# Low parts of the attention's weight slabs written as two pieces of 128x512 on VectorE and four of 128x256 on GpSimd

## The chip, the cores and the metric

The kernel runs on one core of one Trainium2 chip. The metric is the device time of one execution in microseconds (us). The core has TensorE (PE in the profile, with its weight loads shown apart as PEld), VectorE (DVE), ScalarE (ACT), GpSimd (POOL) and the queue that issues transfers (SP). [...] A change of 0.2% (about 4.7 us here) is about what a measurement of this kernel can tell from no change.

## The reference

A trunk of two layers works on 512 latent and 256 context tokens of width 1024. The part that matters here is the differential attention of each layer:

```python
px = hx @ w_in[i]
q_x = px[..., Q_OFF:K_OFF].reshape(B, S, N_HEADS, 2, QK_DIM)
k_x = px[..., K_OFF:V_OFF].reshape(B, S, N_HEADS, 2, QK_DIM)
v_x = px[..., V_OFF:GATE_OFF].reshape(B, S, N_HEADS, V_DIM)
q_x = apply_rope(rmsnorm(q_x, q_norm_g[i]), cos, sin)
k_x = apply_rope(rmsnorm(k_x, k_norm_g[i]), cos, sin)
...
s = jnp.einsum('bqhcd,bkhcd->bhcqk', qi, keys) * scale
p = jax.nn.softmax(s, axis=-1)
w = p[:, :, 0] - lam * p[:, :, 1]
return jnp.einsum('bhqk,bkhv->bqhv', w, vals)
```

Eight heads, two softmax maps a head, everything in float32. Around it lie a conditioning network (adaLN), a convolution branch, a gated merge of both branches with an output projection, and a squared-ReLU MLP of width 4096. Context tokens take part in layer 0 in full; in layer 1 only their keys and values are needed.

## The kernel before

**Numbers in two parts.** A float32 matrix product is made of three faster ones. Each operand X is split into a high part, which ScalarE writes as a rounded copy, and a low part X minus high, a subtraction of two tensors in SBUF. `mm3` (lines 108 to 111) then adds high x high, high x low and low x high in PSUM; these are the matmuls of L109, L110 and L111.

**Weight slabs.** `load_slab` (line 86) brings 1024 rows x 256 columns of a weight matrix into SBUF as a tile of 128 partitions x 8 x 256 (`r_...`), and makes `h_...` and `l_...` from it. It does so in two halves of 128x1024: for each, one ScalarE copy (L76) and one subtraction (L77). The engine of the subtraction is an argument. The attention asks for `both`, a pair: the first half's low part is written by VectorE, the second half's by GpSimd. This holds for the query and key slab of heads 1 to 7 (`qk_slab(i, h, both)`, tiles `l_wqk`) and the value slab of pairs 1 to 3 (`v_slab(i, pr, both)`, tiles `l_wv`): ten slabs in a layer, twenty in all. All other slabs name one engine or none (VectorE).

**One head.** While TensorE runs the attention of head h (`attend`), it also projects head h+1 (`qk_head`) and, for one pair of heads in two, the values (`v_pair`); a list of costs in microseconds (`merge`, the numbers behind `yield`) mixes the two streams. A projected block of 128 tokens goes through ScalarE (`rw`, L542, and its square, L545), VectorE (sum, L547), GpSimd (power -0.5, `rqk`, L548), GpSimd or VectorE (`rw` scaled, L549), GpSimd (`ra` and `rb` for the rotation, L557 and L561), then two sums `dup` (L566: one on GpSimd, one on VectorE), and back to TensorE, which transposes them (`qkT`, L580); L584, L585 and L587 move the result out of PSUM. Scores `S` (L708, L710) live in two PSUM tiles in turn; a third waits until VectorE's maximum (`st`, L712) and ScalarE's exponential (`e`, L715) have read the first. After the combination of both maps (L725), TensorE transposes the weights (`wT`, L738), and ScalarE and VectorE split them (`wth`, `wtl`).

**What sets the order.** The Tile framework draws up the order of each engine's instructions before the kernel runs, by simulating the whole program against modelled durations. Nothing is reordered at run time. Splitting an instruction changes the modelled times, and so the order of others far from it.

Of the kernel before, what the change touches and what calls it, by code (L numbers as in the profile page):

```python
# [10 lines left out]
AF = mybir.ActivationFunctionType  # L11
ALU = mybir.AluOpType
# [34 lines left out]
def f32(ap):  # L47
    return ap.bitcast(F32)
# [3 lines left out]
def trunk_kernel(  # L52
# [6 lines left out]
    nc = tc.nc  # L59
# [15 lines left out]
    def split(hi, lo, src, lo_eng=None):  # L75
        nc.scalar.activation(out=hi, in_=src, func=AF.Copy)  # L76
        return (lo_eng or nc.vector).tensor_tensor(out=lo, in0=src, in1=f32(hi), op=ALU.subtract)  # L77
# [6 lines left out]
    def load_slab(src, name, shape=(KT, 256), lo_eng=None):  # L84
        r = state["tp"].tile([P, *shape], F32, tag="raw", name=f"r_{name}", bufs=state["nraw"])
        if isinstance(src, (list, tuple)):
            for dst, s in src:
                nc.sync.dma_start(r[:, :, dst], s)
        else:
            state["load"] = nc.sync.dma_start(r, src)  # L90
        hi = wpool.tile([P, *shape], F32R, tag="whi", name=f"h_{name}")
        lo = wpool.tile([P, *shape], F32R, tag="wlo", name=f"l_{name}")
        half = shape[0] // 2
        engs = lo_eng if isinstance(lo_eng, tuple) else (lo_eng, lo_eng)
        with ExitStack() as behind:
            for ins in state["behind"]:
                behind.enter_context(tc.issue_after(ins))
            for n, (k, eng) in enumerate(zip((slice(0, half), slice(half, shape[0])), engs)):
                if n and state["turn"]:
                    behind.enter_context(tc.issue_after(state["turn"]))  # L100
                split(hi[:, k], lo[:, k], r[:, k], eng)
        return hi, lo

    def rows(src, col0, ncols):
# [37 lines left out]
    both = nc.vector, nc.gpsimd  # L142
    first = {}

    def qk_slab(i, h, lo_eng=None):
        return load_slab([(slice(0, P), rows(w_in[i], Q_OFF + h * P, P)),
                          (slice(P, 256), rows(w_in[i], K_OFF + h * P, P))], f"wqk{i}_{h}",
                         lo_eng=lo_eng)

    def v_slab(i, pr, lo_eng=None):  # L150
        return load_slab(rows(w_in[i], V_OFF + 256 * pr, 256), f"wv{i}_{pr}", lo_eng=lo_eng)
# [228 lines left out]
    for t in range(NTT):  # L380
        xn = xns[t]
        nc.scalar.activation(out=xn, in_=xrs[t], func=AF.Square, accum_out=rs[:, t : t + 1])
        r = rs[:, t : t + 1]
# [9 lines left out]
    for s in range(2):  # L393
        nc.vector.tensor_tensor(
            out=cvec[:, :, s], in0=L["cols"][:, R_C + 8 * s : R_C + 8 * s + 8],
            in1=sg[:, 8 * s : 8 * s + 8], op=ALU.mult)
# [38 lines left out]
    for i in range(DEPTH):  # L435
# [27 lines left out]
        def conv_load(part, s):  # L463
            return load_slab(rows(wi, (CW if part == "g" else 0) + 256 * s, 256), f"wc{part}{i}_{s}")
# [598 lines left out]
        for s in range(4):  # L1063
# [3 lines left out]
            for g in groups:  # L1067
                W = g.stop - g.start
                for m in range(2):
# [4 lines left out]
                                            op=ALU.mult)  # L1074
# [12 lines left out]
        for cc in range(CT):  # L1087
            for a0, W, t0 in cgr:
                low = nc.vector.tensor_tensor(out=CL[:, cc, t0 : t0 + W],
                                              in0=ca[cc][:, a0 : a0 + W],  # L1090
                                              in1=f32(CH[:, cc, t0 : t0 + W]), op=ALU.subtract)
        normed.append(low.ins)
        mh, ml = [None] * KT, [None] * KT
        for s in range(2):
# [7 lines left out]
            for m in range(4):  # L1102
                mb = 4 * s + m
                for g in groups:
# [5 lines left out]
                                            op=ALU.mult)  # L1110
                rr = {}
                for g in groups:
# [3 lines left out]
                                            op=ALU.add)  # L1116
# [255 lines left out]
```

## Time and profile before

| | us |
|---|---|
| median of 3 runs | 2361.62 (2360.18 to 2363.51) |
| the profiled execution | 2362.06 |
| its span, from first to last instruction | 2360.0 |
| TensorE busy in the span | 2288.2 (97%) |
| VectorE busy | 1468.9 (62%) |
| GpSimd busy | 684.2 (29%) |

The profiled execution lies 0.44 us over the median, and 2.06 us of it lie outside the span. The attention of layer 0 runs from about 50 to 440 us of the span, that of layer 1 from about 1415 to 1760 us; the twenty slabs in question are all made there. Between them lie the merge, the MLP and the conditioning of the next layer.

A row of a timeline gives the start, the duration, the engine, the line, the operation and the tiles, and in square brackets how long the engine stood idle ahead of it and what ended that. Consecutive matmuls overlap, so the bracket, and not the distance between rows, tells TensorE's idle time.

### The profile page before, as it was taken

The numbers are of one execution on the slowest core, as the hardware profiler recorded it, in microseconds if no ns is written. First come the engines' busy times: TensorE is split into PE (matmuls) and PEld (weight loads), VectorE is DVE, ScalarE is ACT, GpSimd is POOL, SyncE is SP. The second block draws the span as 40 slices with busy tenths as digits, with TensorE's granted clock in tenths as the row PEclk, the third lists the DMA queues.
The fourth block names the chain that finished last, engine by engine and source line by source line (L and its number), as shares of the span: only waits on it lengthen the run. The fifth ranks groups of instructions, "written<-read, shape, count | busy, mean of one in ns | idle before, by whom it ended". The sixth has DMA issues, their size and how long they took to land.

```text
span 2360.0 us, 36545 instructions
## 1 busy us (share of the span) xinstructions
PE 2288.2 (97%) x14698; PEld 2051.8 (87%) x14698; DVE 1468.9 (62%) x2583; ACT 993.2 (42%) x1965; POOL 684.2 (29%) x790
## 2 busy tenths in 40 slices
PE   8999999999999999999999998999999999999999
PEld 6999998888888988888888998999877879888887
DVE  6777776699666675655463366776759975433332
ACT  5555654522332353342514345555542333432432
POOL 1866754100000133232322255766610000000000
PEclk9999999999999999999999999999999999999999
DMA  9211111144535223334332211111124324223322
GB/s 313 57 43 31 44 46 44 46 159 131 178 114 188 88 84 125 116 109 132 116 118 71 99 46 56 44 43 44 42 78 130 122 89 126 88 92 95 102 89 72
DMA packets 222570, 224.76 MB, mean 95 GB/s; under 512 B 6256, under 2 KB 212544, under 8 KB 222272
## 3 DMA queue, kind: packets, MB, share of 16 engines
q1 hardware_dynamic: 222400, 222.43, 29.5%
q8 instruction: 115, 1.88, 0.3%
q14 instruction: 55, 0.45, 0.1%
HBM read 208.73 MB, written 13.67 MB: 94 GB/s over the span
## 4 chain that ended last, share of the span: by engine, by line
PE 84%; DVE 7%; ACT 3%; POOL 2%; DMA 1%; issue 1%; SPq 0%; ACTq 0%; DVEq 0%; POOLq 0%
PE r L109 6%; PE r L110 6%; PE r L111 6%; PE f L110 6%; PE f L109 6%; PE f L111 6%; PE gt L109 3%; PE gt L111 3%; PE gt L110 3%; PE qk L109 2%; PE qk L110 2%; PE qk L111 2%; PE v L109 2%; PE v L110 2%; PE v L111 2%; PE o L111 2%
## 5 line engine op out<-in xcount | busy, mean ns | idle before, releaser
L110 PE MATMUL f<-h2l,h_w 128*128 128x512 f32 (+1 forms) x832 | 284.5, 343 | 3.6 <-DVE h2l L328 2.0
L109 PE MATMUL f<-h2h,h_w 128*128 128x512 f32 (+1 forms) x832 | 282.5, 344 | 2.0 <-ACT h2h L76 1.3
L109 PE MATMUL r<-fh,h_w 128*128 128x512 f32 (+1 forms) x832 | 283.9, 342 | 0.0
L110 PE MATMUL r<-fl,h_w 128*128 128x512 f32 (+1 forms) x832 | 283.0, 340 | 0.0
L111 PE MATMUL r<-fh,l_w 128*128 128x512 f32 (+1 forms) x832 | 282.9, 340 | 0.0
L111 PE MATMUL f<-h2h,l_w 128*128 128x512 f32 (+1 forms) x832 | 282.8, 342 | 0.0
L77 POOL TENSOR_TENSOR l_w<-r_w,h_w 128x1024 fp32r<-128x1024 f32 x64 | 156.7, 2471 | 346.9 <-ACT h_w L76 346.9
L76 ACT ACTIVATE h_w<-r_w 128x1024 fp32r<-128x1024 f32 x128 | 128.5, 1051 | 261.3 <-PE r L110 117.2
L263 DVE SCALAR_TENSOR_TENSOR adaac<-ar,cvec,adaac 128x256 f32<-128x256 f32 x336 | 176.7, 579 | 83.9 <-DMA ar<-in_w_ada_dram 62.0
L945 DVE SCALAR_TENSOR_TENSOR cacc<-z,cols,cacc 128x783 f32<-128x783 f32 (+1 forms) x240 | 201.4, 891 | 0.3
L109 PE MATMUL qk<-h_wqk,h1h 128*128 128x256 f32 x640 | 183.6, 289 | 2.1 <-ACT rw L542 1.4
L110 PE MATMUL qk<-l_wqk,h1h 128*128 128x256 f32 x640 | 180.7, 285 | 0.0
L110 PEld LDWEIGHTS f<-h2l,h_w 128*128 128x128 f32 x832 | 158.8, 191 | 22.7 <-POOL h2l L77 2.9
L111 PE MATMUL qk<-h_wqk,h1l 128*128 128x256 f32 x640 | 176.9, 285 | 0.2 <-POOL h1l L77 0.2
L712 DVE TENSOR_REDUCE st<-S 128x1 f32<-128x768 f32 (+1 forms) x160 | 134.7, 846 | 65.4 <-PE S L710 64.4
L1140 DVE SCALAR_TENSOR_TENSOR X<-r,ad,X 128x512 f32<-128x512 f32 (+1 forms) x104 | 64.8, 625 | 176.8 <-PE r L111 176.7
L109 PEld LDWEIGHTS f<-h2h,h_w 128*128 128x128 f32 x832 | 157.0, 191 | 20.4 <-ACT h2h L76 1.7
L111 PEld LDWEIGHTS f<-h2h,l_w 128*128 128x128 f32 x832 | 158.6, 191 | 17.7
L111 PEld LDWEIGHTS r<-fh,l_w 128*128 128x128 f32 x832 | 157.6, 190 | 17.8
L109 PEld LDWEIGHTS r<-fh,h_w 128*128 128x128 f32 x832 | 157.6, 190 | 17.2
L110 PEld LDWEIGHTS r<-fl,h_w 128*128 128x128 f32 x832 | 157.8, 190 | 16.9
L715 ACT ACTIVATE e<-S,st 128x768 f32<-128x768 f32 (+1 forms) x160 | 130.8, 820 | 36.6 <-DVE st L712 36.5
(253 smaller groups left out, 6240.4 us busy)
## 6 DMA issues: line engine op xcount, KB each, us to landing
r_w<-in_w_mlp_dram SPq DMA_DIRECT2D x64, 1024.0 KB, 5.5
ada<-in_w_ada_dram SPq DMA_DIRECT2D x24, 1024.0 KB, 5.4
ar<-in_w_ada_dram SPq DMA_DIRECT2D x48, 512.0 KB, 3.7
r_wqk<-in_w_in_dram SPq DMA_DIRECT2D x32, 512.0 KB, 5.4
r_wg<-in_w_in_dram SPq DMA_DIRECT2D x16, 1024.0 KB, 5.4
r_wv<-in_w_in_dram SPq DMA_DIRECT2D x8, 1024.0 KB, 5.3
r_wao<-in_w_attn_out_dram SPq DMA_DIRECT2D x8, 1024.0 KB, 5.4
r_wo<-in_w_out_dram SPq DMA_DIRECT2D x8, 1024.0 KB, 8.2
```

The source lines that it names most:

```text
L76: nc.scalar.activation(out=hi, in_=src, func=AF.Copy)
L77: return (lo_eng or nc.vector).tensor_tensor(out=lo, in0=src, in1=f32(hi), op=ALU.subtract)
L109: nc.tensor.matmul(ps, sh, mh, start=first, stop=False)
L110: nc.tensor.matmul(ps, sh, ml, start=False, stop=False)
L111: nc.tensor.matmul(ps, sl, mh, start=False, stop=last)
L263: nc.vector.scalar_tensor_tensor(out=a[:, q], in0=r[:, j], scalar=cvec[:, k, q : q + 1], in1=a[:, q], op0=ALU.mult, op1=ALU.add)
L712: nc.vector.tensor_reduce(out=st[:, m : m + 1], in_=S[:, :nkey], axis=AX.X, op=ALU.max, negate=True)
L715: nc.scalar.activation(out=e[:, :nkey], in_=S[:, :nkey], func=AF.Exp, bias=st[:, m : m + 1], accum_out=st[:, 2 + m : 3 + m])
L945: nc.vector.scalar_tensor_tensor(out=ca[cc][:, :CV], in0=zt[cc][:, t : t + CV], scalar=wcol, in1=ca[cc][:, :CV], op0=ALU.mult, op1=ALU.add)
L1140: nc.vector.scalar_tensor_tensor(out=X[:, mb, g], in0=ps[:, :W], scalar=gate[:, s, mb : mb + 1], in1=X[:, mb, g], op0=ALU.mult, op1=ALU.add)
```

## The change

In `load_slab`, slabs whose engines are the pair `both` no longer call `split`. The ScalarE copies stay as they are. VectorE's subtraction of 128x1024 becomes two of 128x512 (two of the slab's eight blocks at a time), GpSimd's becomes four of 128x256 (one block each). The values written are the same.

```diff
             for n, (k, eng) in enumerate(zip((slice(0, half), slice(half, shape[0])), engs)):
                 if n and state["turn"]:
                     behind.enter_context(tc.issue_after(state["turn"]))
-                split(hi[:, k], lo[:, k], r[:, k], eng)
+                if lo_eng is not both:
+                    split(hi[:, k], lo[:, k], r[:, k], eng)
+                    continue
+
+                nc.scalar.activation(out=hi[:, k], in_=r[:, k], func=AF.Copy)
+                step = 2 if n == 0 else 1
+                for k0 in range(k.start, k.stop, step):
+                    p = slice(k0, k0 + step)
+                    eng.tensor_tensor(out=lo[:, p], in0=r[:, p], in1=f32(hi[:, p]),
+                                      op=ALU.subtract)
```

In the program, 20 instructions of VectorE become 40 and 20 of GpSimd become 80; every other instruction is still there. Lines behind the edit move down by nine (L566 becomes L575), and the new subtractions are L109. With few exceptions the pieces of one half stand directly behind each other (`x2`, `x4`). The order around them is drawn up anew, most of all in the attention of layer 0, and at its start in layer 1. Names in the rows below end in a number that the program gives each tile.

**Scores of the first head, TensorE.** `S_0_0_1` and `S_0_1_0` are the second score tile of the first 128 tokens and the first one of the next 128. In layer 0 before:

```order
L708 MATMUL S_0_0_1_1106<-qk_0_708 128x256
L710 MATMUL S_0_0_1_1106<-qk_0_708 128x256
L708 MATMUL S_0_1_0_1159<-qk_0_708 128x512
L710 MATMUL S_0_1_0_1159<-qk_0_708 128x512
L708 MATMUL S_0_1_0_1159<-qk_0_708 128x256
L710 MATMUL S_0_1_0_1159<-qk_0_708 128x256
```

and now:

```order
L717 MATMUL S_0_0_1_1110<-qk_0_708 128x256
L719 MATMUL S_0_0_1_1110<-qk_0_708 128x256
L589 MATMUL qkT_1_0_1184<-cst,dup_1_0_1033 128x128 x4
L118 MATMUL qk_1_3_1192<-h_wqk_1_990,h1h_334 128x256
L119 MATMUL qk_1_3_1192<-l_wqk_1_991,h1h_334 128x256
L120 MATMUL qk_1_3_1192<-h_wqk_1_990,h1l_335 128x256
```

`S_0_1_0` no longer follows at once; the transposes and 18 matmuls of a projection stand between. In layer 1 before:

```order
L708 MATMUL S_0_0_0_15015<-qk_0_14613 128x256
L710 MATMUL S_0_0_0_15015<-qk_0_14613 128x256
L708 MATMUL S_0_0_1_15023<-qk_0_14613 128x256
L710 MATMUL S_0_0_1_15023<-qk_0_14613 128x256
L580 MATMUL qkT_1_0_15075<-cst,dup_1_0_14947 128x128 x4
L109 MATMUL qk_1_3_15105<-h_wqk_1_14908,h1h_9377 128x256
L110 MATMUL qk_1_3_15105<-l_wqk_1_14909,h1h_9377 128x256
L111 MATMUL qk_1_3_15105<-h_wqk_1_14908,h1l_9378 128x256
```

and now:

```order
L717 MATMUL S_0_0_1_15067<-qk_0_14653 128x256
L719 MATMUL S_0_0_1_15067<-qk_0_14653 128x256
L717 MATMUL S_0_1_0_15128<-qk_0_14653 128x512
L719 MATMUL S_0_1_0_15128<-qk_0_14653 128x512
L717 MATMUL S_0_1_0_15128<-qk_0_14653 128x256
L719 MATMUL S_0_1_0_15128<-qk_0_14653 128x256
L589 MATMUL qkT_1_0_15119<-cst,dup_1_0_14991 128x128 x4
```

Here it is the other way round: `S_0_1_0` now follows at once where a whole projection of 24 matmuls stood between.

**The slab of head 2 in layer 1, VectorE and GpSimd.** VectorE before:

```order
L725 SCALAR_TENSOR_TENSOR e_0_1_15090<-e_0_1_15098,st_0_1_15083,e_0_1_15090 128x768
L712 TENSOR_REDUCE st_0_2_15208<-S_0_2_0_15209 128x1
L77 TENSOR_TENSOR l_wqk_2_15461<-r_wqk_2_15457,h_wqk_2_15460 128x1024
L712 TENSOR_REDUCE st_0_2_15208<-S_0_2_1_15217 128x1
L566 TENSOR_TENSOR dup_1_3_15136<-ra_1_3_15137,rb_1_3_15138 128x4x64
L585 TENSOR_TENSOR qk_1_14914<-qkT_1_2_15230,qk_1_14914 128x2x128
L587 TENSOR_TENSOR qk_1_14914<-qkT_1_2_15230,qk_1_14914 64x2x128
```

and now:

```order
L596 TENSOR_TENSOR qk_1_14958<-qkT_1_1_15200,qk_1_14958 64x2x128
L721 TENSOR_REDUCE st_0_2_15252<-S_0_2_1_15261 128x1
L109 TENSOR_TENSOR l_wqk_2_15509<-r_wqk_2_15505,h_wqk_2_15508 128x512 x2
L575 TENSOR_TENSOR dup_1_3_15180<-ra_1_3_15181,rb_1_3_15182 128x4x64
L77 TENSOR_TENSOR wtl_0_0_1_15056<-wT_0_0_1_15194,wth_0_0_1_15055 128x3x128
L594 TENSOR_TENSOR qk_1_14958<-qkT_1_2_15274,qk_1_14958 128x2x128
L596 TENSOR_TENSOR qk_1_14958<-qkT_1_2_15274,qk_1_14958 64x2x128
```

The two halves stand back to back, behind both maxima of `S_0_2` where the whole subtraction stood between them, and `dup_1_3` follows directly. GpSimd at the same place before:

```order
L724 TENSOR_SCALAR es_0_0_15013<-st_0_1_15083 128x1
L557 TENSOR_TENSOR ra_1_3_15137<-rw_1_3_15130,tC_9351 128x256
L561 TENSOR_TENSOR rb_1_3_15138<-rw_1_3_15130,tS_9352 128x4x32 x2
L77 TENSOR_TENSOR l_wqk_2_15461<-r_wqk_2_15457,h_wqk_2_15460 128x1024
L566 TENSOR_TENSOR dup_1_3_15136<-ra_1_3_15137,rb_1_3_15138 128x4x64
L722 TENSOR_TENSOR st_0_2_15208<-st_0_2_15208 128x1
```

and now:

```order
L566 TENSOR_TENSOR ra_1_3_15181<-rw_1_3_15174,tC_9391 128x256
L570 TENSOR_TENSOR rb_1_3_15182<-rw_1_3_15174,tS_9392 128x4x32 x2
L109 TENSOR_TENSOR l_wqk_2_15509<-r_wqk_2_15505,h_wqk_2_15508 128x256 x4
L575 TENSOR_TENSOR dup_1_3_15180<-ra_1_3_15181,rb_1_3_15182 128x4x64
L731 TENSOR_TENSOR st_0_2_15252<-st_0_2_15252 128x1
L733 TENSOR_SCALAR es_0_1_15251<-st_0_2_15252 128x1
```

The four quarters take the place of the one, between `rb_1_3` and `dup_1_3`.

**The slab of head 5 in layer 1, VectorE.** Before:

```order
L725 SCALAR_TENSOR_TENSOR e_3_2_16787<-e_3_2_16795,st_3_2_16780,e_3_2_16787 128x768
L77 TENSOR_TENSOR l_wqk_5_17058<-r_wqk_5_17054,h_wqk_5_17057 128x1024
L712 TENSOR_REDUCE st_3_3_16912<-S_3_3_1_16921 128x1
L566 TENSOR_TENSOR dup_4_3_16755<-ra_4_3_16756,rb_4_3_16757 128x4x64
L585 TENSOR_TENSOR qk_4_16534<-qkT_4_2_16861,qk_4_16534 128x2x128
L587 TENSOR_TENSOR qk_4_16534<-qkT_4_2_16861,qk_4_16534 64x2x128
```

and now:

```order
L734 SCALAR_TENSOR_TENSOR e_3_2_16851<-e_3_2_16859,st_3_2_16844,e_3_2_16851 128x768
L109 TENSOR_TENSOR l_wqk_5_17122<-r_wqk_5_17118,h_wqk_5_17121 128x512 x2
L721 TENSOR_REDUCE st_3_3_16976<-S_3_3_1_16985 128x1
L575 TENSOR_TENSOR dup_4_3_16819<-ra_4_3_16820,rb_4_3_16821 128x4x64
L594 TENSOR_TENSOR qk_4_16598<-qkT_4_2_16925,qk_4_16598 128x2x128
L596 TENSOR_TENSOR qk_4_16598<-qkT_4_2_16925,qk_4_16598 64x2x128
```

Only the subtraction itself has changed; what stands ahead of it and behind it is the same. The slabs of heads 3 and 7 lie in the same surroundings.

## Rows read from the trace of the kernel before

**Rows 1.** The page's first part: busy us of each engine, share, instructions.
```profile
PE 2288.2 (97%) x14698; PEld 2051.8 (87%) x14698; DVE 1468.9 (62%) x2583; ACT 993.2 (42%) x1965; POOL 684.2 (29%) x790
```

**Rows 2.** Windows: stretch, length, busy of PE, PEld, DVE, ACT, POOL; clock; DMA.
```profile
50.00:440.00 390.00, 378.86 (x2919) 363.34 (x2918) 283.78 (x563) 220.91 (x546) 239.25 (x348) 0.99 0.16 47
...
1415.00:1760.00 345.00, 325.09 (x2390) 306.23 (x2389) 232.92 (x404) 187.11 (x416) 203.72 (x280) 0.98 0.16 49
```

**Rows 3.** Waits of PE, 55 to 430 us: total us, times, longest.
```profile
PE S L708 <- ACT e L715: 3.7, 3, 1.8
...
PE qkT L580 <- POOL dup L569: 2.0, 4, 1.3
PE wT L738 <- DVE wtl L77: 1.7, 3, 0.9
```

**Rows 4.** Waits of PE, 1420 to 1760 us.
```profile
PE v L109 <- DVE qk L587: 5.9, 3, 2.5
PE v L109 <- DVE vl L77: 3.0, 2, 2.5
```

**Rows 5.** Tile l_wqk: who waited for it (us, times).
```profile
who waited for it (us, times):
  PEld adaps L221: 0.3, 1
```

**Rows 6.** Line L77 by form: ns min/median/max, first and last start.
```profile
L77 POOL TENSOR_TENSOR l_w<-r_w,h_w x64: 2379/2402/2697, 816.9 to 1349.3; 128x1024 fp32r<-128x1024 f32 x64
...
L77 DVE TENSOR_TENSOR h1l<-ar,h1h x20: 681/684/694, 625.4 to 1886.1; 128x512 fp32r<-128x512 f32 x20
...
L77 DVE TENSOR_TENSOR l_wqk<-r_wqk,h_wqk x14: 1207/1222/1773, 61.7 to 1662.9; 128x1024 fp32r<-128x1024 f32 x14
L77 POOL TENSOR_TENSOR h1l<-nu_n,h1h x12: 733/740/912, 1369.8 to 1416.3; 128x256 fp32r<-128x256 f32 x12
```

**Rows 7.** Tile dup, its VectorE form: ns min/median/max, first and last start.
```profile
L566 DVE TENSOR_TENSOR dup<-ra,rb x64: 404/426/2586, 64.6 to 1707.5; 128x256 f32<-128x256 f32 x64
```

**Rows 8.** Timelines of POOL, DVE and PE around 1452 us, and DVE at 66.
```profile
1452.13 2.40 POOL L77 TENSOR_TENSOR l_wqk<-r_wqk,h_wqk 128x1024 fp32r<-128x1024 f32 x1
...
1452.22 2.59 DVE L566 TENSOR_TENSOR dup<-ra,rb 128x256 f32<-128x256 f32 x1
...
1459.40 0.44 PE L109 MATMUL v<-h_wv,h1h 128*128 128x256 f32 x1 [2.51 <-DVE vl L77]
...
66.37 2.54 DVE L566 TENSOR_TENSOR dup<-ra,rb 128x256 f32<-128x256 f32 x1
```

**Rows 9.** The chain that ended last, 1579 to 1583 us: start, us, what.
```profile
1579.22 1.48 DVE l_wqk L77
1580.70 0.87 DVE st L712
1581.57 0.53 DVE dup L566
...
1582.44 0.44 DVE qk L587
...
1583.02 0.55 PE v L109
```

**Rows 10.** Timeline of POOL at 153 to 159 us, and at 1578 us.
```profile
153.56 1.50 POOL L549 TENSOR_TENSOR rw<-rw,rqk 128x256 f32<-128x256 f32 x1
...
156.52 2.41 POOL L77 TENSOR_TENSOR l_wqk<-r_wqk,h_wqk 128x1024 fp32r<-128x1024 f32 x1
...
1578.44 2.57 POOL L561 TENSOR_TENSOR rb<-rw,tS 128x128 f32<-128x128 f32 x2
```

**Rows 11.** Timeline of PE: four matmuls that waited.
```profile
163.21 0.33 PE L580 MATMUL qkT<-cst,dup 128*128 128x128 f32 x1 [0.25 <-POOL dup L569]
...
90.19 0.50 PE L708 MATMUL S<-qk 128*128 128x512 f32 x1 [1.84 <-ACT e L715]
...
385.30 0.58 PE L708 MATMUL S<-qk 128*128 128x256 f32 x1 [1.45 <-ACT e L715]
...
1451.38 0.50 PE L708 MATMUL S<-qk 128*128 128x512 f32 x1 [1.38 <-ACT e L715]
```

## The prediction

> **What bounds the kernel now.** I read the busy shares of the page first. TensorE is busy for 97% of the span, and no other engine for more than 62% [rows 1]. So only time in which TensorE stands idle can be won, and only work that makes it stand idle can cost. The windows then tell how much of that lies where the twenty slabs are made: in the attention of layer 0 TensorE is idle for 390 - 378.86 = 11.1 us, in that of layer 1 for 345 - 325.09 = 19.9 us [rows 2]. That is 31 us, 1.3% of the span, and the change can win no more. GpSimd is busy for 239.25 of 390 us in the first stretch and 203.72 of 345 us in the second [rows 2]: some 60%, with long work in single file.
>
> Next I read whom TensorE waits for in these stretches. In layer 0 it is ScalarE's exponential (3.7 us), GpSimd's `dup` (2.0 us for its context form) and VectorE's `wtl` (1.7 us) [rows 3]; in layer 1 VectorE's last step of emptying a `qkT` tile (5.9 us in three waits) and `vl` (3.0 us in two) [rows 4]. The low parts themselves are not among them: the only wait for `l_wqk` in the whole trace is 0.3 us [rows 5]. Writing them in pieces so that a matmul could start on the first piece is thus worth nothing. What the pieces can alter is what stands behind them in the queues of VectorE and GpSimd, what these two engines do to each other, and the order that is drawn up anew.
>
> **What the two engines do to each other.** A VectorE `dup` of 128x256 takes 426 ns at the median, and 2586 ns at most [rows 7]. The longest one began 0.09 us after a GpSimd `l_wqk` of 2.40 us and took 2.59 us; its twin at 66.37 us took 2.54 us in the same position [rows 8]. It also goes the other way: a GpSimd `rw` of 128x256 took 1.50 us, and two small `rb` took 2.57 us, each beside a VectorE `l_wqk` [rows 10]. So the one that comes second waits for most of the other's instruction, and a shorter instruction is a shorter wait. [...]
>
> **The change part by part.** *More work.* Subtractions of the new shapes stand elsewhere in the trace: 128x256 on GpSimd takes 740 ns, 128x512 on VectorE 684 ns, against 2402 and 1222 ns for 128x1024 [rows 6]. A slab costs GpSimd 4 x 0.740 - 2.402 = 0.56 us more and VectorE 2 x 0.684 - 1.222 = 0.15 us more; over twenty slabs 11.2 and 2.9 us. Nearly all of it lies beside matmuls, since both engines are idle for a quarter or more of the time; it counts where a slab stands on the way to a wait of TensorE, and those places I take one by one. [...]
>
> *A: the long stall of VectorE.* The `dup` that took 2.59 us stands in a chain on VectorE that ends with `vl` and a wait of TensorE of 2.51 us [rows 8]. Against a piece of 0.74 us it waits for at most that: 2.16 us of stall become at most 0.74, and the wait shrinks by 1.4 us. In the new order `dup_1_3` still stands at the slab there, with the four quarters beside it. Bounds: 0, if what stands behind it is late anyway, to -2.2 us, if the whole stall goes. I take -1.4. The twin at 66 us releases no wait and counts 0.
>
> *B: VectorE's slab ahead of a wait.* Before the matmul at 1583.02 us the chain runs through `l_wqk` (1.48 us), a maximum, `dup` and the emptying of `qkT` [rows 9]. It is one of the three waits of rows 4, and the order there is unchanged. Two halves cost 0.15 us more at least. At that time GpSimd's `rb` is waiting for its turn (2.57 us for two, rows 10) and can now slip in between the halves; that adds at most what a larger GpSimd piece takes, 0.74 us. So 0.15 to 0.89 us each, three times: 0.4 to 2.7 us. Near the lower end, since the second half stands ready when the first ends and `rb` needs only a part of that: 0.3 each, +0.9 in all.
>
> *C: GpSimd's slab ahead of a wait.* In layer 0 TensorE waited 0.25 us at 163.21 us for a `dup` [rows 11] that stands behind `rw`, a slab's low part and another `rw` in GpSimd's queue [rows 10]; the same wait with the same length comes once more, at 345.84 us. The slab is 0.56 us longer, and `rw`, which lost 1.50 - 0.74 = 0.76 us to the VectorE slab, would lose about half. Each comes to +0.56 - 0.38 = +0.2: +0.4 in all. Bounds: -1.5 (all of 0.76 won twice) to +1.1 (only the longer slab, twice).
>
> *D: the new order of the scores.* The three longest waits for the exponential are 1.84, 1.45 and 1.38 us [rows 11]. The first is the pair of score tiles of the first head in layer 0 that stood side by side and now has a projection between; the second is a context tile of head 6, which stood two rows of the program behind the tile ahead of it and now stands 36 behind. Against them, in layer 1 the first head's pair has come together, so that the wait of 1.84 us, as layer 0 had it, should appear there in place of the 1.38. That is -1.84 - 1.45 + 1.84 - 1.38 = -2.8 if nothing else is late behind. But the next to wait there are `qkT` and `wT`, which already wait in rows 3, so I keep rather less than half: -1.2. Bounds -2.8 to +1.8 (only the new wait).
>
> *The rest of the order.* Some 1,100 of 14,386 rows of TensorE stand elsewhere, nearly all in layer 0. The order is made from modelled durations and knows nothing of the mutual waits above. I see no sign in it either way and put it at 0.
>
> **The sum.** -1.4 + 0.9 + 0.4 - 1.2 = -1.3 us. The profiled execution took 2362.06 us, 2.06 of them outside the span, so this gives 2360.8; against the median, which is 0.44 lower, 2360.3. The bounds together are -6.5 to +5.6: 2355.1 to 2367.2.
>
> **The rivals.** *Faster.* The mutual waits are the true cause of most of what TensorE waits for, and shorter holds free both engines. The waits of rows 3 and 4 come to 7.4 and 8.9 us; if half goes, that is -8.2 us and 2353.4. For it: stretched operations stand in the chains of rows 8 to 10. Against it: a `dup` of 2.54 us at 66 us cost TensorE nothing, and in rows 9 the halved slab still stands ahead of the same four steps.
>
> *Slower.* GpSimd's queue becomes the bound of layer 0's heads. It decides from the point at which a slab's extra 0.56 us exceeds the slack of the `dup` behind it; at 163.21 us that slack is used up already, since TensorE waited 0.25 us there [rows 11]. If all ten slabs of layer 0 come to that, they cost 5.6 us, and with the upper bound of B in layer 1 the total is +8.3: 2369.9. For it: every step of a head's keys passes through GpSimd's one queue, and its work grows by 11.2 us. Against it: it is still idle for 390 - 239 = 151 us there.
>
> *No relief.* The pieces stand back to back, so the second might take its turn before the engine that waits, and holds would be as long as before. Then A is 0, B 0.4, C 1.1 and D as above: +0.3, 2361.9, which is no difference that can be measured.
>
> **How the numbers follow.** The forecast has a chance of 0.38, no relief 0.12, faster 0.26, slower 0.24. A measurement tells 0.2%, 4.7 us, from no change: faster means under 2356.9, slower over 2366.3. The forecast's lower end lies a little beyond the first bound (0.04) and its upper one beyond the second (0.02), so faster has 0.30, within 0.2% has 0.44 and slower 0.26. I take 2360.3. Signs are spread, so the range takes in most of both rivals: 2352 to 2370; the likeliest case alone spans 2355.1 to 2367.2.
>
> **What would show it.** A: no VectorE `dup` over about 1.3 us, and the wait near 1459 us under 1.5 us. B: the three waits for `qkT` in layer 1 still there, 2.5 to 3.3 us long (the shortest 1.0 to 1.8). C: GpSimd's quarters at 0.70 to 0.75 us, its busy time up by 8 to 12 us. D: no wait for the exponential near 90 us, one near 1.8 us at the first head of layer 1. If TensorE's idle time in layer 0 moves by more than 4 us either way, the new order, and not the pieces, has set the result; if that in layer 1 falls by more than 4 us, the mutual waits were worth more than I gave them.

## The result, and the profile after

The changed kernel took 2370.52 us (median; 2367.3 to 2377.66) against 2363.92 us of the kernel before on the same chip: a ratio of 1.0028, with a 95% interval of 1.002 to 1.0036. It is slower by 6.6 us, clear of the noise; the forecast was 1.3 us faster.

The profiled execution is the longest of the 18 behind that median (2377.66 us), so a second profile of the same kernel, from the first experiment (e1), stands beside it; it is called the repetition below. The page's line of busy times in the repetition (compare rows 1):

```profile
PE 2285.1 (97%) x14698; PEld 2044.5 (86%) x14698; DVE 1476.4 (62%) x2603; ACT 994.1 (42%) x1965; POOL 691.7 (29%) x850
```

In the repetition (span 2367.2 us) TensorE is idle for 2367.2 - 2285.1 = 82.1 us; before it was 2360.0 - 2288.2 = 71.8 us [rows 1]. So there are 10.3 us more of idle time, against 3.1 us less of busy time (the granted clock was 0.991 in this execution and 0.987 in the one profiled before). Where are they? The windows of the attention, first layer 0's in the first profile of the changed kernel, then both layers' in its repetition (columns as in rows 2):

```profile
50.00:440.00 390.00, 371.24 (x2830) 353.31 (x2829) 290.27 (x565) 216.35 (x534) 241.68 (x375) 0.97 0.16 48
```

```profile
50.00:440.00 390.00, 377.61 (x2894) 358.66 (x2893) 286.84 (x570) 220.81 (x544) 243.37 (x378) 0.99 0.16 47
1415.00:1760.00 345.00, 325.17 (x2423) 306.06 (x2421) 236.40 (x416) 189.58 (x422) 214.12 (x316) 1.00 0.16 49
```

In layer 1 the idle time is 19.8 us, as before (19.9). In layer 0 it is 18.8 us in the first profile and 12.4 us in the second, against 11.1 before. The difference of these two is one instruction. Timelines in the first profile, of VectorE and then of TensorE:

```profile
73.85 8.23 DVE L575 TENSOR_TENSOR dup<-ra,rb 128x256 f32<-128x256 f32 x1
```

```profile
82.23 1.09 PE L589 MATMUL qkT<-cst,dup 128*128 128x128 f32 x4 [4.73 <-DVE dup L575]
```

A VectorE addition, of a kind with a median of 0.62 us in this profile, stood for 8.23 us while GpSimd worked on without a pause, and TensorE waited 4.73 us for it, and 1.72 us more at the next transposes. No `dup` of the repetition or of any other profile exceeds 2.59 us, so this is an accident of that execution and not the loss of 6.6 us.

The loss lies where I had not looked: behind the attention. Waits of TensorE in the kernel before, 840 to 890 us and 1860 to 1950 us (columns as in rows 3):

```profile
PE f L110 <- DVE h2l L328: 1.8, 1, 1.8
...
PE yc L118 <- ACT ch L1052: 1.4, 2, 1.0
PE yc L118 <- DVE g L1109: 0.7, 1, 0.7
PE ya L110 <- DVE h1l L77: 0.5, 1, 0.5
```

and in the repetition of the changed kernel (its lines are 9 higher):

```profile
PE adaps L281 <- DVE adaac L272: 4.1, 1, 4.1
...
PE yc L127 <- ACT ch L1061: 2.3, 1, 2.3
PE ya L119 <- DVE h1l L77: 1.5, 2, 1.2
PE ya L118 <- DVE g L1082: 1.5, 1, 1.5
PE yc L127 <- DVE g L1118: 1.0, 1, 1.0
```

The first place is a new wait of 4.1 us. It is at the end of layer 0, in the MLP, where the modulation of layer 1 (`adaps`) is computed between the output matmuls `f`. What TensorE's queue holds there, before and after (place in the queue, line, operation, tiles):

```
5161 L110 MATMUL f_0_5_0_9806<-h2l_8457,h_w_0_0_2_9757 128x512
5162 L272 MATMUL adaps_2_10262<-cst,adaac_2_10129 128x128 x4
```

```
5135 L281 MATMUL adaps_2_10302<-cst,adaac_2_10169 128x128 x2
...
5160 L281 MATMUL adaps_2_10302<-cst,adaac_2_10169 128x128
5161 L118 MATMUL f_0_4_0_9803<-h2h_8496,h_w_0_0_2_9797 128x512
...
5165 L281 MATMUL adaps_2_10302<-cst,adaac_2_10169 128x128
```

Two of the four transposes now stand 27 places further ahead. They need `adaac`, and VectorE has that no sooner than before. Timelines of VectorE and TensorE in the kernel before, then of VectorE, GpSimd and TensorE in the repetition:

```profile
860.46 5.42 DVE L263 SCALAR_TENSOR_TENSOR adaac<-ar,cvec,adaac 128x256 f32<-128x256 f32 x8 [1.26 <-DMA ar<-in_w_ada_dram]
...
865.77 0.60 PE L272 MATMUL adaps<-cst,adaac 128*128 128x128 f32 x4
```

```profile
860.29 7.47 DVE L272 SCALAR_TENSOR_TENSOR adaac<-ar,cvec,adaac 128x256 f32<-128x256 f32 x8 [1.06 <-DMA ar<-in_w_ada_dram]
...
862.43 5.05 POOL L77 TENSOR_TENSOR l_w<-r_w,h_w 128x1024 fp32r<-128x1024 f32 x2 [2.05 <-ACT h_w L76]
...
865.30 0.44 PE L281 MATMUL adaps<-cst,adaac 128*128 128x128 f32 x2 [4.13 <-DVE adaac L272]
```

Before, `adaac` was written up to 865.88 us and `adaps` came just then, with no wait. Now TensorE comes to it at 861.2 us and stands still, with all that is behind in its queue.

About half of this wait is one VectorE instruction that stands behind GpSimd: the seventh of the eight `adaac` took 2.57 us instead of 0.48, beside a `l_w` of 2.53 us that GpSimd had begun 0.24 us ahead of it. In the first profile the seventh began 0.02 us ahead of that `l_w` and took 0.48 us, and the wait was 1.8 us:

```profile
873.87 0.44 PE L281 MATMUL adaps<-cst,adaac 128*128 128x128 f32 x2 [1.77 <-DVE adaac L272]
```

So the place costs a wait of 1.8 to 4.1 us, according to which of the two engines is first.

The second place is the end of layer 1's attention and its convolution. From 55 us ahead of the first gate matmul to the last matmul of `yc`, the windows of the kernel before and of the repetition:

```profile
1732.00:1944.00 212.00, 201.42 (x903) 164.08 (x902) 171.82 (x249) 73.43 (x112) 10.78 (x12) 0.97 0.33 108
```

```profile
1734.00:1951.00 217.00, 201.34 (x893) 163.11 (x892) 171.81 (x245) 72.40 (x108) 9.85 (x10) 0.96 0.32 102
```

TensorE's and VectorE's work is the same to 0.1 us, and the stretch is 5 us longer. The chain of waits there, before and in the repetition (start, us, what; of its rows some of the layer norm's sums `tot`, its matmuls `ln` and the matmuls `yc`):

```profile
1887.48 0.70 DVE tot L1014
1888.23 1.13 PE ln L1017 x2
...
1932.02 2.13 PE yc L118 x8
```

```profile
1890.46 0.60 DVE tot L1023
...
1905.11 0.86 PE ln L1026 x2
...
1939.08 2.13 PE yc L127 x8
```

Both queues were drawn up anew there. `ln` needs the third `tot`. Before, that is the row at 1887.48 us; in the repetition the row at 1890.46 us is the second one, and the third is not on the chain:

```profile
1897.34 0.68 DVE L1023 TENSOR_TENSOR tot<-tot,cacc 128x512 f32<-128x512 f32 x1
```

In VectorE's queue, two additions of `g` and two slabs `l_wao` now stand ahead of it; in TensorE's, `ln` has moved from ahead of the output block `ya_2` to ahead of `ya_4`. So `ln` comes 17 us later: some 10 of them are VectorE's, and for the other 7 its operand was ready and its place in TensorE's queue held it. `yc`, for which its result is needed, comes 7.1 us later, 2 of which it brought along from further ahead. Which of these moves costs the 5 us was not tried one by one.

### The profile page after: what moved, and what is told of

Same layout as the page of the kernel before. It is cut to its first block, busy times and chain, and to the rows that moved or that the text cites. A ratio compares the mean times of both kernels' runs of the same rounds, so it can differ in the third digit from the quotient of the medians.

```text
span 2375.9 us, 36611 instructions
## 1 busy us (share of the span) xinstructions
PE 2291.3 (96%) x14698; PEld 2049.8 (86%) x14698; DVE 1486.5 (63%) x2603; ACT 994.8 (42%) x1965; POOL 693.4 (29%) x850
## 4 chain that ended last, share of the span: by engine, by line
PE 82%; DVE 8%; POOL 5%; ACT 3%; issue 2%; DMA 1%; SPq 0%; ACTq 0%; POOLq 0%; DVEq 0%
PE r L118 6%; PE r L119 6%; PE r L120 6%; PE f L119 6%; PE f L118 6%; PE f L120 6%; PE gt L118 3%; PE gt L120 3%; PE gt L119 3%; PE qk L118 2%; PE qk L119 2%; PE qk L120 2%; PE o L120 2%; PE o L119 2%; PE o L118 2%
## 5 line engine op out<-in xcount | busy, mean ns | idle before, releaser
L77 POOL TENSOR_TENSOR l_w<-r_w,h_w 128x1024 fp32r<-128x1024 f32 x64 | 157.0, 2475 | 348.1 <-ACT h_w L76 348.1
```

## The experiments

Each kernel was timed in turn with the kernel before on the same chip. Ratios to the kernel before, with 95% intervals:

| run | slabs | order | ratio | interval |
|---|---|---|---|---|
| e1 | both in pieces | changed | 1.0028 | 1.0012 to 1.0044 |
| e2 | both in pieces | before | 1.0009 | 1.0000 to 1.0017 |
| e3 | whole | changed | 1.0055 | 1.0042 to 1.0068 |
| e5 | both in pieces | changed, two places as before | 0.9992 | 0.9982 to 1.0001 |
| e6 | whole | before, two places as changed | 1.0020 | 1.0009 to 1.0030 |
| e13 | both in pieces | changed, first place as before | 1.0020 | 1.0011 to 1.0030 |
| e14 | both in pieces | changed, second place as before | 1.0008 | 0.9997 to 1.0019 |
| e8 | GpSimd's in pieces | before | 1.0015 | 1.0004 to 1.0027 |
| e11 | VectorE's in pieces | before | 1.0081 | 1.0068 to 1.0093 |
| e12 | GpSimd's in pieces | changed | 1.0049 | 1.0035 to 1.0063 |
| e9 | whole, buffers as changed | changed | 1.0085 | 1.0071 to 1.0099 |
| e10 | whole, buffers as with pieces | before | 1.0059 | 1.0047 to 1.0071 |
| e4 | pieces in layer 1 alone | the scheduler's own | 0.9987 | 0.9974 to 1.0000 |
| e7, e15 | pieces in layer 1 alone | before, layer 1's heads as changed | 0.9989, 0.9983 | 0.9980 to 0.9998, 0.9974 to 0.9991 |
| e16 | pieces in layer 1 alone | before | 1.0002 | 0.9991 to 1.0013 |

**Is it the order or the pieces?** The change does both, since the scheduler orders the instructions by its own reckoning of their times. To hold one while the other changes, the order of each engine was read from the built program and forced on another one by a chain of issue-order edges; a table holds the five orders, one an engine:

```diff
     with _tile.TileContext(nc, schedule_with_timeline_sim=True) as tc:
         trunk_kernel(tc, *args)
+        _pin(tc)
...
+    for part in zlib.decompress(base64.b85decode("".join(_ORDER))).decode().split("|"):
+        n, last = 0, None
+        for d in part.split(","):
+            n += int(d)
+            if last is not None:
+                tc.add_manual_dep(traced[n], last.name, info, reason="pinned order")
+            last = traced[n]
```

e1 is the changed kernel again; e2 has its slabs and the order before, e3 the slabs before and its order. That the edges cost little by themselves is seen in e2 and e16, which have them and lie within 0.1% of the kernel before.

> The changed kernel once more, unaltered, for a second profile. In the first one a VectorE addition for the first head (written at L575, 73.85 us) stands 8.23 us while thirteen GpSimd instructions go past it, and TensorE idles 4.7 and 1.7 us behind it. If that stand belongs to the order of the changed kernel (theory order), it is there again within half a microsecond and the time is again 1.002 to 1.0036 of the kernel before. If it was an accident of one execution (theory accident), the addition takes 0.4 to 1.0 us, the first score matmul of layer 0 comes near 85 us instead of 90.9, and the span is 2367 to 2370 us.

> The short pieces as in the changed kernel, but every engine issues in the order of the kernel before; the pieces of a slab part stand together where the one instruction stood. Theory order (what costs is the new order that the scheduler made of the pieces): 0.997 to 1.000 of the kernel before, layer 0's attention as long as before within 1.5 us. Theory work (the pieces themselves cost, by 11 us more on GpSimd, 3 us on VectorE and more turns at the shared port): 1.002 to 1.0036, as the changed kernel.

> The one 128x1024 instruction each as in the kernel before, but every engine issues in the order of the changed kernel. Theory order: 1.002 to 1.004 of the kernel before, the loss at the start of layer 0's attention (55 to 110 us). Theory work: 1.000 within 0.001.

e1 gave 1.0028 again (1.0014 by the medians, since its twelve executions scatter, up to 2382.7 us), and its profile has no stand of 8.23 us: accident, not order. e2 gave 1.0009, a little above what theory order had named, and e3 1.0055, well above. So the order costs 0.55% by itself, with the buffers that it brings (see below), and the theory that the pieces' work costs is out: in the order before they cost 0.0 to 0.17%, and in the changed order they give some of the loss back (from 1.0055 to 1.0028). My place for the loss, 55 to 110 us, holds only a small part of it: TensorE is idle there for 5.0 us in e3 and for 2.7 in the kernel before. e3 has the wait of 4.2 us at `adaps` and the same idle time around the convolution.

**Where in the order?** The two orders differ in four stretches, each complete in itself: layer 0's attention, the place at 861 us, layer 1's start and heads, and its last head with the convolution. So they can be mixed by stretch, with the same few lines and another table.

> The changed kernel with all its pieces and its order in both layers' attention, but at two places behind them every engine issues as in the kernel before: around 861 us, where three of the second layer's modulation matmuls (adaps) stand ahead of the last block's fifth and sixth output matmuls and TensorE waits 4.13 us, and from layer 1's last head to the end of its convolution (1740 to 1945 us), where TensorE idles 15.7 us instead of 10.6. Theory order at two places: the 4.1 and most of the 5.0 us go, so 7 to 9 us less than the changed kernel, 0.9985 to 1.0005 of the kernel before. Rival (the loss lies in the attention, and idle time removed here comes back later): 1.0015 to 1.003.

> The kernel before, no pieces, with the changed kernel's order at those two places alone (around 861 us, and from layer 1's last head to the end of its convolution). Theory order at two places: 7 to 9 us more than the kernel before, 1.0025 to 1.004. Rival (the loss lies in the attention): 1.000 to 1.001.

> The changed kernel with all its pieces and its order, but around 861 us alone (the modulation matmuls adaps) as the kernel before. Theory order at two places: TensorE's wait of 4.1 us for adaac is gone (at most 1.3 left), the idle time from layer 1's last head to the end of its convolution stays at 15 to 16 us; 1.0005 to 1.002 of the kernel before. If the whole loss sat here: 0.999 to 1.000; if the wait came back elsewhere: 1.002 to 1.0036.

> The same with the other place back, from layer 1's last head to the end of its convolution. Theory order at two places: idle time there 10 to 11 us instead of 15 to 16, the wait of 4.1 us at 861 us stays; 1.0005 to 1.002 of the kernel before.

With both places back the changed kernel is at 0.9992 instead of 1.0028: 8.5 us less (6 to 11 by the two intervals). With both places moved the kernel before, nothing else altered, is at 1.0020, 4.7 us more (2 to 7); that is under what I had named. One place back at a time gives 1.0020 and 1.0008, so the first is worth some 2 us and the second some 5, each give or take 3, which by the times alone does not tell the first from nothing. The profiles do: from the first `yc` of layer 0 to its first `r` (714.3 and 906.4 us in the repetition) TensorE takes 192.1 us in the repetition and in e14, 192.8 in e6, but 187.3 in the kernel before, 187.1 in e13 and 188.9 in e5. The waits go as the places do. TensorE between 840 and 890 us in e6 and then in e5:

```profile
PE adaps L272 <- DVE adaac L263: 4.3, 1, 4.3
```

```profile
PE f L119 <- DVE h2l L337: 1.8, 1, 1.8
...
PE adaps L281 <- DVE cols L173: 0.6, 1, 0.6
```

Whole slabs in the order before get the wait when the place is moved, and pieces lose it when it is put back. The pieces have no part in it.

**What do the pieces themselves do?** Half of the change at a time, and then none of it but a side effect:

```diff
-                step = 2 if n == 0 else 1
+                step = half if n == 0 else 1     # e8, e12: GpSimd's alone
...
-                step = 2 if n == 0 else 1
+                step = 2 if n == 0 else half     # e11: VectorE's alone
```

> GpSimd's part in four pieces, VectorE's part whole, every engine in the order of the kernel before. If GpSimd's whole instruction is what holds VectorE up ahead of heads 3, 5 and 7 of layer 1 (theory mutual), the waits of 2.48 us there are 0.77 and 0.97 as with both parts in pieces, and the time is 0.9995 to 1.001. If VectorE's halves do it, the waits stay at 2.48 us.

Theory mutual fell, and the other branch held: the waits ahead of heads 3, 5 and 7 that rows 4 show did not shrink with GpSimd's pieces. TensorE's waits for `v`, 1490 to 1740 us, in e8:

```profile
PE v L118 <- DVE qk L596: 6.0, 3, 2.5
```

With both parts in pieces (e2) two of the three are other waits, and the one that is left, 0.98 us before, is longer:

```profile
PE v L118 <- ACT rwc L613: 2.3, 4, 0.8
...
PE v L118 <- DVE vl L77: 1.9, 2, 1.0
PE v L118 <- DVE qk L596: 1.6, 1, 1.6
```

The programs tell why. `v`, `qk`, `qkT`, `kcT` and others take turns in two PSUM buffers, and which one a tile gets is settled when the order is made, by the same reckoning. With VectorE's pieces 26 tiles of layer 1's later heads have the other buffer than before, although the order is the same; with GpSimd's alone none has. A `v` that follows `kcT` into its buffer waits for ScalarE's `rwc` (0.77 us at 1502.65 us of the repetition); one that follows `qkT` waits for VectorE (2.48 us at 1666.74 us of the kernel before). So e9 and e10 have whole slabs and the other buffers, which 64 columns written twice bring about:

```diff
                 split(hi[:, k], lo[:, k], r[:, k], eng)
+                if lo_eng is both and n == 0 and name[:4] in ("wqk1", "wv1_"):
+                    j = slice(k.stop - 1, k.stop)
+                    eng.tensor_tensor(out=lo[:, j, :64], in0=r[:, j, :64], in1=f32(hi[:, j, :64]),
+                                      op=ALU.subtract)
```

> Whole slabs in the order of the changed kernel, as in the run whole_order_after, but VectorE subtracts the last 64 columns of its part of each of layer 1's slabs a second time. That lengthens the part a little in the scheduler's reckoning, and 154 PSUM tiles get the other of their pool's buffers, just those that the changed kernel has; nothing is in pieces. Theory buffers (what the pieces give back under the changed order, 9 us between whole_order_after and the changed kernel, comes from which PSUM buffer a tile was given, not from shorter turns at the port): 1.002 to 1.0036, and the waits of 2.48 us ahead of the v matmuls of layer 1 at about 1507, 1591 and 1676 us are pairs of 0.77 and 0.97. Theory turns: 1.0045 to 1.0065, as whole_order_after, and the waits stay at 2.48.

> The same repeated 64 columns in the order of the kernel before: whole slabs, and the 26 PSUM tiles of layer 1 (heads 5 to 7) that the pieces move to the other buffer have it here too. Theory buffers: the waits of 2.48 us near 1581 and 1664 us are pairs of 0.77 and 0.97 as in pieces_order_before, with no spell at the lower clock behind them; 0.998 to 1.0005. Theory turns: both stay at 2.48 us, 1.000 to 1.001.

> VectorE's part in two pieces, GpSimd's whole, order of the kernel before; the 26 tiles have the other buffer. Theory buffers: as the run before in this call, 0.998 to 1.0005, with the same pairs of waits; the difference to quarters_order_before (1.0015) is the two waits with their spells and GpSimd's dearer pieces. Theory turns: the waits shrink here and not in the run before.

> GpSimd's part in four pieces, VectorE's whole, order of the changed kernel; the PSUM buffers are those of whole_order_after. Theory buffers: 1.0045 to 1.0065 with three waits of 2.48 us, as whole_order_after. Theory turns (GpSimd's shorter turns free VectorE): 1.002 to 1.0036.

Both theories were too simple. The waits of 2.48 us did go where the buffers changed, with no piece anywhere (e9, e10), so their end is the buffers' work. But the time rose, to 1.0085 and 1.0059, and so it did with VectorE's pieces alone (1.0081), which bring the same buffers. Other waits took their place. TensorE, 1490 to 1740 us, in e10 and in e11:

```profile
PE wT L742 <- DVE wtl L77: 4.8, 2, 2.4
```

```profile
PE wT L747 <- DVE wtl L77: 4.4, 2, 2.2
PE v L118 <- DVE qk L596: 3.2, 1, 3.2
```

The rows behind the wait of 3.2 us, which ends at 1515.94 us, GpSimd and VectorE in e11:

```profile
1511.94 2.79 POOL L109 TENSOR_TENSOR l_wqk<-r_wqk,h_wqk 128x1024 fp32r<-128x1024 f32 x1
...
1512.45 2.56 DVE L575 TENSOR_TENSOR dup<-ra,rb 128x256 f32<-128x256 f32 x1
```

GpSimd's whole slab has come ahead of VectorE's `dup`, which stands behind it for 2.56 us. In the kernel before, the same `dup` began 0.63 us ahead of the slab and had its turn first:

```profile
1498.68 0.94 DVE L566 TENSOR_TENSOR dup<-ra,rb 128x256 f32<-128x256 f32 x1
...
1499.31 2.57 POOL L77 TENSOR_TENSOR l_wqk<-r_wqk,h_wqk 128x1024 fp32r<-128x1024 f32 x1
```

What made it late is VectorE's own part just ahead of it: 1.22 us before, 1.82 us in two pieces (e11), 1.22 and 0.63 us in e10, where the 64 columns are one instruction more. In layer 1's attention six `dup` stand for over 2 us in e10 and in e11, and one before. So e9 and e10 change VectorE's queue too, and what the buffers are worth by themselves stays open. The line of `dup` on VectorE in that stretch (ns least/median/most), in e11 and with both parts in pieces (e2):

```profile
L575 DVE TENSOR_TENSOR dup<-ra,rb x24: 407/796/2562, 1497.2 to 1730.5; 128x256 f32<-128x256 f32 x24
```

```profile
L575 DVE TENSOR_TENSOR dup<-ra,rb x22: 415/772/1019, 1493.3 to 1707.2; 128x256 f32<-128x256 f32 x22
```

So GpSimd's short pieces do what a shorter turn promises, 1.02 us at most instead of 2.56, but mostly against stalls that VectorE's pieces (or the 64 columns) bring about; in the kernel before only two `dup` stood that long [rows 7, 8]. (The "port" in the expectations of e2 and e9 is my name for what lies behind these stands; the runs show how long they last, and not what the two engines share.) Taken together the two halves are near nothing in the order before (e2), and each alone costs. That e12 stayed at 1.0049 with its three waits of 2.5 us fits this. VectorE's pieces alone in the changed order were not run, so it is not shown what brings the changed kernel back from 1.0055 to 1.0028; and why GpSimd's pieces alone cost 0.15% (e8) I cannot say.

**Is there something to keep?** Pieces in layer 1's slabs alone, first as the scheduler orders it, then in mixed orders.

```diff
-                if lo_eng is not both:
+                if lo_eng is not both or name[2:3] == "0" or name[3:4] == "0":
```

> The pieces only in layer 1's slabs; layer 0's stay whole, and the scheduler orders anew. TensorE's order then differs from that of the kernel before in 703 of 14384 places instead of 3315, none of them ahead of layer 1. Theory order: layer 0 as before, so 0.998 to 1.0005. Theory work: about half of the loss, 1.001 to 1.002.

> Pieces in layer 1's slabs alone; order of the kernel before everywhere but at the start of layer 1 and in its heads up to the sixth, where it is the changed kernel's. Theory: layer 0 as before (0), the modulation matmuls and the convolution as before (0), and layer 1's heads as in the changed kernel: the 2.48 us waits ahead of heads 3, 5 and 7 become pairs of 0.77 and 0.97 with no spell at the lower clock behind them. Together 2 to 5 us less than the kernel before, 0.998 to 0.9993. Rival (pieces give nothing but under the changed order): 1.000 to 1.001.

> The kernel of the run layer1_pieces_order_mixed once more (pieces in layer 1 alone, changed order at layer 1's start and heads alone), since it was 0.9989 with 0.998 to 0.9998. A real gain gives 0.998 to 0.9995 again; no gain gives 0.9995 to 1.001.

> Pieces in layer 1 alone, every engine in the order of the kernel before. Theory: layer 0 as before, layer 1's attention as in pieces_order_before, where TensorE idled 1.7 us less in the heads and 1.8 us more ahead of them: 0.9985 to 1.0005. If the gain of the mixed run needs the changed order, this is 0.0005 to 0.002 above it.

The mixed kernel is faster than the kernel before: 0.9989 and, timed again, 0.9983, which is 2.6 and 4.0 us (0.5 to 4.7 and 2.1 to 6.1), less than the 0.2% named at the start. With the order before the same pieces give nothing (1.0002). So the gain needs the changed order of layer 1's heads. Whether it needs the pieces too is not shown, since whole slabs were not run in the mixed order; e4, where the scheduler's own order differs from that before only from layer 1 on, is near it. TensorE's waits from 1430 to 1740 us in e15 show the pairs of 0.77 and 0.97 us in place of rows 4, and the wait at the first head (`S`):

```profile
PE S L717 <- ACT e L724: 3.6, 2, 2.8
PE v L118 <- DVE vl L77: 3.4, 4, 1.0
PE v L118 <- ACT rwc L613: 3.1, 5, 0.8
```

In the kernel before, the clock was lower behind the two waits of 2.48 us, too: after the one that ends at 1583.02 us the granted clock was 0.64 of full speed from 1583 to 1587 us, and after the one that ends at 1666.74 us it was 0.60 from 1667 to 1671 us. In the repetition of the changed kernel, which has no such wait there, it was 1.00 from 1582 to 1590 us and from 1664 to 1672 us.

## Why the prediction was wrong, point by point

**What bounds the kernel: right**, and it was the key to the answer. The time went where TensorE idles, by 10.3 us more, and no other engine became the bound. But I then read only the two attention stretches. The change could win no more than their 31 us; it could lose anywhere.

**The step that failed: "the rest of the order ... I put it at 0."** It measured 8.5 us (6 to 11) between the changed kernel and e5, where only the two late places are put back: a wait of up to 4.1 us at `adaps`, and 5 us more of idle time around the convolution. I had looked at how many rows moved and where most of them are (layer 0's attention), and not at the few that moved behind it. How far each place could cost was to be read from the trace of before: TensorE came to the place where `adaps` now stands at 861 us, and VectorE had `adaac` at 865.9. "I see no sign in it either way" was true of the count and false of the rows. The count itself was low by another way of counting: place by place, 3315 of 14384 differ, 703 in layer 1 even with pieces there alone (expectation of e4). It also missed that the same reckoning hands out PSUM buffers.

**A, the long stall: right on the stall, wrong on its worth.** No `dup` of layer 1 in the changed kernel exceeds 1.02 us. But with the order held (e16) the wait behind it is still 2.2 us instead of 2.51, a gain of 0.3 and not 1.4; it only goes with the new order (0.8 us in the repetition). TensorE, 1405 to 1500 us, in e16:

```profile
PE v L118 <- DVE vl L77: 2.7, 2, 2.2
```

**B, the waits for `qkT`: wrong, by the buffers.** They were to grow by 0.3 us each; in the changed kernel each became a pair of 0.77 and 0.97 us. With GpSimd's pieces alone the two long ones stayed at 2.5.

**C, GpSimd's slab: right.** Its pieces have a median of 0.74 us, its busy time rose by 7.5 us in the repetition, a little under the 8 to 12 foreseen, and TensorE's waits in layer 0 for the context form of GpSimd's `dup` went from 2.0 us [rows 3] to 2.3 in the repetition: +0.3 where I had 0.4. TensorE's waits there, 55 to 430 us:

```profile
PE S L717 <- ACT e L724: 2.9, 6, 1.5
...
PE qkT L589 <- POOL dup L578: 2.3, 4, 1.2
PE S L717 <- DVE qk L596: 1.2, 1, 1.2
```

**D, the scores: the direction right, the size wrong.** The wait at 90 us went and one came at layer 1's first head, as foreseen, but with 2.8 us instead of 1.84. In layer 0 the waits for the exponential went from 3.7 us [rows 3] to 2.9, at layer 1's first head from 1.38 [rows 11] to 2.8: +0.6, where I had -1.2; and a wait of 1.2 us for VectorE's `qk` took the place of the first.

**The sum without the failed step came out near, by luck**: e5, the changed kernel with its attention as the prediction reckoned it, is 1.9 us faster (4.3 faster to 0.2 slower), against 1.3, but the terms were off by more than that and cancelled. The lower bound was also added up wrongly: with B's own 0.4 us it is -6.1 and 2355.5 us, not -6.5 and 2355.1. **The rivals:** "slower" gave nearly the right time, 2369.9, by a mechanism that isn't there; GpSimd's queue did not become the bound (e2). "No relief" is out, since no `dup` of the repetition exceeds 1.02 us. "Faster" asked for 8.2 us, and the best kernel here (e15) gained 4.0. My own tripwire, idle time in layer 0 moving by more than 4 us, pointed to the order as the cause, but watched the wrong stretch: it moved by 1.3 us in the repetition.

## What to carry to other kernels

Where a scheduler orders by modelled times, an edit of a few instructions is two changes: the instructions, and a new order (and new buffers) everywhere behind them. Price every stretch in which the order differs, not the one that was edited: for each matmul that moved ahead, look up in the old trace when its operand was ready. And keep the two apart when measuring, by pinning one order on both kernels; here the new order alone cost 0.55%, twice the whole effect, and the pieces alone 0.09%, each with the buffers that came with it.

## What the runs showed of the hardware that was not expected

VectorE and GpSimd hold each other up with no semaphore between them. In the kernel before, 23 `adaac`, whose two tensors lie in SBUF and whose median is 0.48 us, began while a GpSimd `l_w` ran, and all 23 ended 0.28 to 0.29 us behind its end. Of the 81 `wtl`, which read `wT` from PSUM, and the 88 maxima `st`, which read `S` from PSUM, that began while a GpSimd instruction ran, none took 0.08 us more than the shortest of its kind. An instruction that was held up had its turn at the end of the GpSimd instruction then running, if it began early enough. Over the profiles of all kernels here, some 2300 VectorE instructions that were held up (by 0.08 us or more beyond the shortest of their kind) saw one GpSimd instruction end; 119 saw two end (in the kernel before 116 and 4, in the changed kernel 142 and 8), and each of them had begun 0.110 us or less ahead of the first end. None of the 2300 had begun so late: the latest began 0.197 us ahead. That 0.197 is a mark of the selection and not of the chip, since an instruction that begins later and has its turn is held up by less than 0.08 us; with a bound of 0.04 us the latest is at 0.164. So of those held up the turn was missed by all that began 0.110 us or less ahead, and where between 0.110 and 0.164 us it is decided is not shown. Which of the two began first does not settle it alone: the 119 waited for a second instruction that had not begun when they did.

One of all these instructions fits neither: the `dup` of 8.23 us began 0.355 us ahead of an end and let thirteen GpSimd instructions pass, until GpSimd stopped for lack of work. What sets it apart I do not know. It happened once, and the 6.45 us that TensorE waited for it are most of the 7.14 us by which that execution exceeds the median.
